# Making two of three mixed input blocks of a hybrid decoder layer in the heads' stage, and giving single weight parts their own buffers

## The chip, the cores and the metric

The kernel runs on one core of one Trainium2 chip. The metric is device time in microseconds (us) for one execution of the program. A core has five engines that this document names as the profile does: PE (the matrix multiplier, with PEld for its weight loads), DVE (vector), ACT (scalar, activation functions), POOL (general purpose; here it issues small transfers) and SP (issues the large transfers). Each engine runs its own instructions strictly in the order of its queue and waits on semaphores for the others.

## The reference

One decoder layer over 256 tokens of width 2048, all in float32. Cut to what matters here:

```python
h = _rmsnorm(x, pre_norm_g)                                  # 256 x 2048
(q_a, c_kv, k_rope, z_mla, c_in, b_gate, c_gate, z_conv,
 g_mla, g_conv) = split(h @ w_in)                            # seven of the parts are 2048 wide
...                                                          # 16 heads of latent attention
attn = attn * silu(z_mla);  y_mla = attn @ w_o_mla
u = c_gate * c_in;  conv = sum(conv_w[k] * shifted(u, k) for k in range(3))
y_conv = (b_gate * conv * silu(z_conv)) @ w_o_conv
merged = sigmoid(g_mla) * y_mla + sigmoid(g_conv) * y_conv   # the "gates" stage: g_mla, g_conv
x = x + _rmsnorm(merged @ w_out, post_norm_g)
```

## The kernel before

**Every product is three products.** The kernel keeps float32 accuracy with matrix products on rounded operands: each operand is split into `hi` (rounded, made by ACT, L282) and `lo` (the rest, made by DVE as `src - hi`, L283; both in `split_act`). A product is hi·hi + hi·lo + lo·hi, three matmuls of 128x512 on PE (`product`). The input x lives split in `x_both` (16 blocks of 128 columns, hi beside lo) for the whole run.

**Weights stream.** SP loads units of 128x2048 into `raw` (three buffers), ACT and DVE split them in halves of 1024 into `whi` and `wlo` (five buffers each), PE consumes them. `plan` lists the units in the order of use; `ahead`/`take` run the splitting one unit ahead and the loading three ahead.

**Stages.** First the latents, then the *heads' stage* (16 heads; each is interleaved with a quarter of the convolution's channels, so that PE always has `cv` matmuls to run), then the *gates and merge* stage: four products of 256x2048 by 2048x2048 (n = 0: g_mla, n = 1: g_conv, n = 2: w_o_mla, n = 3: w_o_conv), each in two halves c = 0, 1 of the output's columns, called blocks (n, c) here; then the output projection.

**The gates' blocks use seven products instead of eight.** A block runs over eight pairs k of x's blocks; each pair is a 2x2 by 2x2 block product. For pairs 0, 3 and 5 (`FAST`) of n = 0 and 1, `fast_block` makes it with seven products, which need sums of weight parts (`split_seven`: `ts` the sums, `th`/`tl` their hi and lo) and *mixed input blocks*, four differences of x's blocks for each pair (`mixed`: `xr` is x put together again from hi and lo, `xm` the four differences, `mix` their hi and lo). Products go into the PSUM banks p1, q5, q7, q6, p2, q3, q4 (the profile's `p`, `q`, `d`). Block (0, 0) runs the pairs in the order 1, 2, 4, 0, 6, 3, 5, 7 and treats only pairs 0 and 3 as fast; it is the first block after the heads' stage. The mixed blocks of pairs 0, 3 and 5 are made once, in block (0, 0), by `between(i)` before the pairs at places 1, 3 and 5, in two `ev` buffers, and are used in blocks (0, 0) to (1, 1). Units are numbered in the names: 116 is pair 0 of block (0, 0), 117 pair 6, 118 pair 3, and 121 and 124 are pairs 0 and 3 of block (0, 1). `split_seven` puts three quarters of a unit into one full and one half-filled buffer of `whi` and of `wlo`.

**What sets the order.** PE's order is the program's. On DVE and ACT a list scheduler places the instructions when the kernel is built, by its own estimate of times, but each engine then runs its queue in that fixed order.

**Small transfers.** In the heads' stage POOL issues the transposes through DRAM (`far<-via`, then `p<-far` for a head's probabilities; `far<-cw` and `at_f<-far` for gates; `cw<-cwr_dram` for the convolution's taps). `cw` is a ring of two buffers of 128x512 that stays open until n = 1. [...]

Of the kernel before, what the change touches and what calls it, by code (L numbers as in the profile page):

```python
# [11 lines left out]
F32 = mybir.dt.float32  # L12
# [3 lines left out]
ALU = mybir.AluOpType  # L16
# [68 lines left out]
def tile_layer(ctx: ExitStack, tc: tile.TileContext, xw, w0, xb, x, pos, pvec, post_g, wc, wz, wcv, wkr, wqk, wqr, wv, cwr, wd, wo, out):  # L85
# [130 lines left out]
        splits[i] = parts  # L216

    def split_seven(i, t):
        hi, hi2 = (wpool.tile([P, HALF], F32R, name=f"whi{i}_{j}", tag="whi", bufs=5) for j in range(2))
        lo, lo2 = (wpool.tile([P, HALF], F32R, name=f"wlo{i}_{j}", tag="wlo", bufs=5) for j in range(2))  # L220
        ta, tb = (sums(f"ts{i}_{j}") for j in range(2))
        ha, hb = (sums_hi(f"th{i}_{j}") for j in range(2))
        la, lb = (sums_lo(f"tl{i}_{j}") for j in range(2))
        plus = lambda o, a, b: nc.vector.tensor_tensor(o, a, b, op=ALU.add)
        two = lambda a: a.rearrange("p (j c) -> p j c", j=2)
        plus(two(ta[:, :]), two(t[:, :HALF]), t[:, 3 * R :].unsqueeze(1).to_broadcast([P, 2, R]))
        plus(tb[:, :R], ta[:, :R], t[:, R:HALF])
        plus(tb[:, R:], tb[:, :R], t[:, HALF : 3 * R])
        split_act(hi[:, :], lo[:, :], t[:, :HALF])
        split_act(hi2[:, :R], lo2[:, :R], t[:, HALF : 3 * R])  # L230
        split_act(ha[:, :], la[:, :], ta[:, :])
        split_act(hb[:, :], lb[:, :], tb[:, :])
        f = lambda a: (a[:, :R], a[:, R:])
        (b11, b22), (t1, t3), (t2, t4) = (list(zip(f(h), f(l))) for h, l in ((hi, lo), (ha, la), (hb, lb)))
        return {"b11": b11, "b22": b22, "b21": (hi2[:, :R], lo2[:, :R]), "t1": t1, "t2": t2, "t3": t3, "t4": t4}

    def ahead(i, raw=3, split=1):
        while done["raw"] < min(i + raw, len(plan)):
# [42 lines left out]
    def split_act(hi, lo, src, keep=False, later=False):  # L281
        a = nc.scalar.activation(hi, src, AF.Copy)  # L282
        b = nc.vector.tensor_tensor(lo, src, hi.bitcast(F32), op=ALU.subtract)  # L283
        if keep:

            tc.keep_in_program_order(a)
        if keep or later:
            tc.keep_in_program_order(b)
# [31 lines left out]
    main = ctx.enter_context(ExitStack())  # L320
    hp = main.enter_context(tc.tile_pool(name="hp", bufs=1))
    x_both = hp.tile([P, KD, 2 * S], F32R, name="x_both")
    cstack, astack = (main.enter_context(ExitStack()) for _ in range(2))
    cv_pool = cstack.enter_context(tc.tile_pool(name="cv_pool", bufs=1, side="right"))
    cv_f = cv_pool.tile([P, KD, S], F32, name="cv_f")
# [21 lines left out]
    def temp(name, shape=(P, S), dt=F32, bufs=2, tag=None):  # L347

        tag, n = tag or name.rstrip("0123456789_"), shape[-1]
        if n % LINE == 0:  # L350
            return (lp if tag in ("cw", "mv1x", "mv2x") else bp).tile(list(shape), dt, name=name, tag=tag, bufs=bufs)
        return bp.tile([P, -(-n // LINE) * LINE], dt, name=name, tag=tag, bufs=bufs)[:, :n]
# [84 lines left out]
    def rows(dst):  # L437
        tc.keep_in_program_order(nc.vector.tensor_tensor(dst, dst, r_x[:, :], op=ALU.mult))
# [201 lines left out]
    def group_v(v):  # L640
# [9 lines left out]
        groups["v", v] = vv  # L650
        yield

    def make(i, j, *more):
        return {"a": group_a, "r": group_r, "v": group_v}[i](j, *more)

# [187 lines left out]
    def score(h, later=False):  # L843
        made_here = scores(h)

        def rest():
            ps_by_head[h], come = made_here(later)
            coming.append(come)

        return rest if later else rest()  # L850

    for h in range(H):
        v, at = divmod(h, HV)

        if at == 0:
            for i in range(4):
                gates(v, i)
                if v == 0 and i == 0:
                    ckv_come()
                elif v == 0 and i == 1:  # L860
                    next(table_parts)
                    key_rope()
                elif v == 0 and i == 2:
                    latent_split("qa", qa, "q_g")
                elif v and i == 0:
                    arrive()
                elif v and i == 1:
                    pt = turn(ps_by_head.pop(h - 1))
                    next(tap)
                elif v and i == 2:  # L870
                    o = values(h - 1, pt)
                    next(o)
                    finish_all(make("v", v))
                    score(h)
                    finish_all(o)
            if v:
                next(tap)
            else:
                latent_split("ckv", ckv, "kv_g")
            gates_done(v)  # L880
            if v:
                arrive()
        if h == 0:

            ahead(u_grp["r", 0])
            for i in first:
                finish_all(make(*i))
        if at == 2:

            score(h)  # L890
        channels(h, 0)
        if h == 0:
            score(h)
        if at in (1, 3) and h < H - 1:
            arrive()
        if at == 0:
            coming.append(gates_turn(v, 0))
        channels(h, 1)
        if at == 0:
            arrive()  # L900
            coming.append(gates_turn(v, 1))
        else:
            pt = turn(ps_by_head.pop(h - 1))
        if h == H - 2:
            score(h + 1)

        if at == 2 or h == H - 1:
            next(tap)
        if at == 2:
            arrive()  # L910
        channels(h, 2)


        steps = [make(*i, *([at == 3] if i[0] == "a" else [])) for i in made[h]]
        if at:
            steps.append(values(h - 1, pt))
        for g in steps:
            next(g)
        if not at:
            arrive()  # L920
            if v:
                coming.append(channels_join(v - 1, 0))
        ahead_by_one = at in (0, 2) and h < H - 2
        if ahead_by_one:
            rest = score(h + 1, later=True)
        finish_all(*steps[::-1])
        if h == H - 1:
            pt = turn(ps_by_head.pop(h))
        channels(h, 3)
        if ahead_by_one:  # L930

            rest()
        if at == 2 or h == H - 1:
            next(tap)
        while len(coming) > ahead_by_one and h < H - 1:
            arrive()
        if h == H - 1:
            finish_all(values(h, pt))
        if at == 3:
            coming.append(channels_join(v, 1))  # L940
        if at == 1:
            tap = taps(v, 1)
            next(tap)
        elif at == 3 and h + 1 < H or h == H - 2:
            tap = taps(v, 0)
            next(tap)
# [20 lines left out]
        gate[n][t] = sp.tile([P, D], F32, name=f"g{n}_{t}")  # L967

    gate_tile(1, 0)
    mix = {k: sp.tile([P, 2, 4 * P], F32R, name=f"mix{k}") for k in FAST[::-1]}  # L970
    sums_lo("home")
    for t in range(NT):
        gate_tile(0, t)

# [25 lines left out]
    def split_group(place, src, c):  # L1000
        for t in range(NT):
            split_turned(src[:, c, t, :], place, c, t)

    def mixed(k):
        tmp = evens(f"xr{k}")
        f = tmp[:, :].rearrange("p (j s) -> p j s", j=2)
        ks = slice(2 * k, 2 * k + 2)
        nc.vector.tensor_tensor(f, x_both[:, ks, :S].bitcast(F32), x_both[:, ks, S:].bitcast(F32), op=ALU.add)
        raw = evens(f"xm{k}")
        a11, a21, a12, a22 = (f[:, j, t * P : (t + 1) * P] for j in range(2) for t in range(2))  # L1010
        m7, m5, m6, m3 = (raw[:, j * P : (j + 1) * P] for j in range(4))
        minus = lambda o, a, b: nc.vector.tensor_tensor(o, a, b, op=ALU.subtract)
        minus(m7, a21, a11)
        minus(m5, a21, a22)
        minus(m6, a11, m5)
        minus(m3, a12, m6)
        split_act(mix[k][:, 0, :], mix[k][:, 1, :], raw[:, :])

    def mix_part(k, j):
        return tuple(mix[k][:, o, j * P : (j + 1) * P] for o in range(2))  # L1020
# [77 lines left out]
    for n in range(2):  # L1098
        if n:
            lstack.close()  # L1100
            last_gate = spool.enter_context(tc.tile_pool(name="last_gate", bufs=1))
            gate[1][1] = last_gate.tile([P, D], F32, name="g1_1")
        for c in range(2):

            def between(i):
                if n == c == 0 and i in (1, 3, 5):
                    mixed(FAST[i // 2])
                if n == c == 1 and i in (2, 4, 6):
                    split_group(at_place, at_t, i // 2 - 1)

            outs = [[gate[n][t][:, columns(c, j)] for j in range(2)] for t in range(NT)]
            fast_block(n, c, x_part, outs, between)
            for t in range(NT):
                for o in outs[t]:
                    nc.scalar.activation(o, o, AF.Sigmoid, scale=r_col[:, t : t + 1])
# [231 lines left out]
```

## Time and profile before

| | us |
|---|---|
| median of 3 runs (1033.6 to 1034.96) | 1034.54 |
| the profiled execution, its own time | 1034.48 |
| span of its profile (first to last instruction) | 1032.7 |
| PE busy | 1022.6 (99% of the span) |
| DVE busy | 747.4 (72%) |
| ACT busy | 543.9 (53%) |
| POOL busy | 179.0 (17%) |

How to read the views: a row of the timeline has the start and the duration in us, the engine, the line, the operation, output<-input, and how many such instructions stand together (xN); the brackets behind it give the idle time of that engine just before, and what ended it. A row of the waits has the waiting operation, what it waited for, the total in us, the number of waits and the longest. A row of the windows has, for a stretch of the span, the busy time of each engine with the number of instructions in brackets, the clock granted to PE as a share of full speed, the busy share of the DMA engines and GB/s. PE's matmuls overlap in the pipeline, so a matmul's duration (0.39 us) is longer than the step from one to the next.

### The profile page before, as it was taken

The numbers are of one execution on the slowest core, as the hardware profiler recorded it, in microseconds if no ns is written. First come the engines' busy times: TensorE is split into PE (matmuls) and PEld (weight loads), VectorE is DVE, ScalarE is ACT, GpSimd is POOL, SyncE is SP. The second block draws the span as 40 slices with busy tenths as digits, with TensorE's granted clock in tenths as the row PEclk, the third lists the DMA queues.
The fourth block names the chain that finished last, engine by engine and source line by source line (L and its number), as shares of the span: only waits on it lengthen the run. The fifth ranks groups of instructions, "written<-read, shape, count | busy, mean of one in ns | idle before, by whom it ended". The sixth has DMA issues, their size and how long they took to land.

```text
span 1032.7 us, 12827 instructions
## 1 busy us (share of the span) xinstructions
PE 1022.6 (99%) x4651; PEld 851.5 (82%) x4651; DVE 747.4 (72%) x1062; ACT 543.9 (53%) x764; POOL 179.0 (17%) x344
## 2 busy tenths in 40 slices
PE   9999999999999999999999989999999999999998
PEld 7888888888888888888888868888888888888886
DVE  7588777787777777777877798898875554756572
ACT  7665545655456454564555546555654443344451
POOL 4540421104301223112133120000000000214000
PEclk9999999999999999999999989999999999999999
DMA  9775866568665676757676755555555555577852
GB/s 357 276 260 202 279 205 234 213 201 282 218 246 197 220 263 211 273 192 244 229 269 222 260 183 178 226 206 204 204 198 182 193 202 196 197 258 246 344 184 81
DMA packets 44528, 233.26 MB, mean 226 GB/s; under 512 B 7953, under 2 KB 10513, under 8 KB 21553
## 3 DMA queue, kind: packets, MB, share of 16 engines
q1 hardware_dynamic: 32400, 199.67, 54.8%
q0 software_dynamic: 11632, 29.48, 8.8%
q10 hardware_dynamic: 432, 3.29, 0.8%
q8 instruction: 36, 0.59, 0.2%
q14 instruction: 28, 0.22, 0.1%
HBM read 215.66 MB, written 12.58 MB: 221 GB/s over the span
## 4 chain that ended last, share of the span: by engine, by line
PE 97%; DVE 2%; DMA 0%; ACT 0%; issue 0%
PE cv L90 34%; PE sq L90 17%; PE q L90 8%; PE z L90 8%; PE out L90 8%; PE p L90 4%; PE d L90 2%; PE kn L90 2%; PE qa L90 2%; PE qn L90 2%; PE vv L90 2%; PE ckv L90 2%; PE sc L90 1%; PE qr L90 1%; PE o L90 1%; DVE wlo L283 1%
## 5 line engine op out<-in xcount | busy, mean ns | idle before, releaser
L283 DVE TENSOR_TENSOR wlo<-raw,whi 128x1024 fp32r<-128x1024 f32 (+1 forms) x370 | 431.8, 1179 | 202.8 <-ACT whi L282 195.4
L282 ACT ACTIVATE whi<-raw 128x1024 fp32r<-128x1024 f32 (+1 forms) x372 | 373.2, 1021 | 376.0 <-PE cv L90 116.9
L90 PE MATMUL cv<-whi,x_both 128*128 128x512 f32 x1024 | 319.8, 389 | 0.0
L90 PEld LDWEIGHTS cv<-whi,x_both 128*128 128x128 f32 x1024 | 192.3, 188 | 39.4
L90 PE MATMUL cv<-wlo,x_both 128*128 128x512 f32 x512 | 199.6, 390 | 0.0
L90 PE MATMUL sq<-whi,x_both 128*128 128x512 f32 x384 | 118.8, 389 | 0.0
L90 PEld LDWEIGHTS cv<-wlo,x_both 128*128 128x128 f32 x512 | 96.1, 188 | 19.5 <-DVE wlo L283 0.2
L90 PEld LDWEIGHTS sq<-whi,x_both 128*128 128x128 f32 x384 | 72.1, 188 | 15.0
L90 PE MATMUL z<-whi,x_both 128*128 128x512 f32 x256 | 80.0, 389 | 0.0
L90 PE MATMUL out<-whi,x_both 128*128 128x512 f32 x256 | 79.0, 389 | 0.0
L90 PE MATMUL sq<-wlo,x_both 128*128 128x512 f32 x192 | 74.7, 389 | 0.0
L367 POOL DMA_DIRECT2D far<-g x32 | 17.4, 551 | 322.5 <-DVE g L1138 289.9
L367 POOL DMA_DIRECT2D far<-via x64 | 35.2, 556 | 179.2 <-DVE via L359 178.9
L90 PEld LDWEIGHTS out<-whi,x_both 128*128 128x128 f32 x256 | 48.1, 188 | 9.9
L90 PEld LDWEIGHTS z<-whi,x_both 128*128 128x128 f32 x256 | 48.1, 188 | 9.9
L90 PE MATMUL q<-whi,x_both 128*128 128x512 f32 x168 | 55.1, 389 | 0.0
L90 PE MATMUL z<-wlo,x_both 128*128 128x512 f32 x128 | 49.8, 389 | 0.0
L90 PE MATMUL out<-wlo,x_both 128*128 128x512 f32 x128 | 49.8, 389 | 0.0
L90 PE MATMUL p<-whi,x_both 128*128 128x512 f32 x128 | 46.6, 391 | 0.0
L90 PEld LDWEIGHTS sq<-wlo,x_both 128*128 128x128 f32 x192 | 36.0, 188 | 7.4
L367 POOL DMA_DIRECT2D far<-cw x48 | 26.1, 551 | 79.1 <-DVE cw L359 79.1
L90 PE MATMUL sq<-whi,cv_first 128*128 128x512 f32 x128 | 39.7, 389 | 0.0
(253 smaller groups left out, 1433.0 us busy)
## 6 DMA issues: line engine op xcount, KB each, us to landing
raw<-wcv_dram SPq DMA_DIRECT2D x64, 1024.0 KB, 5.9
raw<-wd_dram SPq DMA_DIRECT2D x64, 1024.0 KB, 4.8
raw<-wz_dram SPq DMA_DIRECT2D x16, 1024.0 KB, 4.8
raw<-wo_dram SPq DMA_DIRECT2D x16, 1024.0 KB, 5.0
raw<-wqk_dram SPq DMA_DIRECT2D x8, 1024.0 KB, 6.1
cw<-cwr_dram POOLq DMA_DIRECT2D x24, 256.0 KB, 6.2
raw<-wc_dram SPq DMA_DIRECT2D x4, 1024.0 KB, 10.4
raw<-wv_dram SPq DMA_DIRECT2D x4, 1024.0 KB, 4.8
```

The source lines that it names most:

```text
L90: return tc.keep_in_program_order(nc.tensor.matmul(*a, **kw))
L282: a = nc.scalar.activation(hi, src, AF.Copy)
L283: b = nc.vector.tensor_tensor(lo, src, hi.bitcast(F32), op=ALU.subtract)
L367: tc.keep_in_program_order(queue.dma_start(out=f[i], in_=m))
```

## The change

Four edits:

1. `mixed` moves up in the code, takes its scratch from the caller, and is called for pairs 0 and 3 in heads 5 and 9 (`h in (HV + 1, 2 * HV + 1)`), with two `f` buffers and one `cw` buffer as scratch. x is now put together in two instructions of 128x256 rather than one of 128x512.
2. The buffers `mix0` and `mix3` (2 x 4096 bytes per partition) therefore live in `hp` through the heads' stage; the room comes from `dynamic_dma_scratch_size=8192`.
3. The third mix (pair 5, first needed in block (0, 1)) stays in block (0, 0) but moves from place 5 to place 6.
4. The half-filled `whi`/`wlo` buffers of `split_seven` are replaced by `ph`/`pl`, 128x512, two buffers each. The room is that of the two mixes, which left this pool.

```diff
     def split_seven(i, t):
-        hi, hi2 = (wpool.tile([P, HALF], F32R, name=f"whi{i}_{j}", tag="whi", bufs=5) for j in range(2))
-        lo, lo2 = (wpool.tile([P, HALF], F32R, name=f"wlo{i}_{j}", tag="wlo", bufs=5) for j in range(2))
+        hi, lo = (wpool.tile([P, HALF], F32R, name=f"{o}{i}", tag=o, bufs=5) for o in ("whi", "wlo"))
+        hi2, lo2 = part_hi(f"ph{i}"), part_lo(f"pl{i}")
...
-        split_act(hi2[:, :R], lo2[:, :R], t[:, HALF : 3 * R])
+        split_act(hi2[:, :], lo2[:, :], t[:, HALF : 3 * R])
...
     x_both = hp.tile([P, KD, 2 * S], F32R, name="x_both")
+    mix = {k: hp.tile([P, 2, 4 * P], F32R, name=f"mix{k}") for k in FAST[:2]}
...
+    def mixed(k, rows, raw):
+        xs = [rows(j) for j in range(2)]
+        for j, x in enumerate(xs):
+            h, l = (x_both[:, 2 * k + j, o : o + S].bitcast(F32) for o in (0, S))
+            nc.vector.tensor_tensor(x, h, l, op=ALU.add)
+        a11, a21, a12, a22 = (x[:, t * P : (t + 1) * P] for x in xs for t in range(2))
+        m7, m5, m6, m3 = (raw[:, j * P : (j + 1) * P] for j in range(4))
+        minus = lambda o, a, b: nc.vector.tensor_tensor(o, a, b, op=ALU.subtract)
+        minus(m7, a21, a11)
+        minus(m5, a21, a22)
+        minus(m6, a11, m5)
+        minus(m3, a12, m6)
+        split_act(mix[k][:, 0, :], mix[k][:, 1, :], raw)
...
         if h == H - 2:
             score(h + 1)
+        if h in (HV + 1, 2 * HV + 1):
+            mixed(FAST[v - 1], lambda j: temp("f")[:, :], temp("cw", (P, 512), bufs=2)[:, :])
...
-    mix = {k: sp.tile([P, 2, 4 * P], F32R, name=f"mix{k}") for k in FAST[::-1]}
-    sums_lo("home")
+    mix[FAST[2]] = sp.tile([P, 2, 4 * P], F32R, name=f"mix{FAST[2]}")
+    part_hi, part_lo = (ring(tag, F32R, R) for tag in ("ph", "pl"))
+    for r in (part_hi, part_lo, sums_lo):
+        r("home")
...
             def between(i):
-                if n == c == 0 and i in (1, 3, 5):
-                    mixed(FAST[i // 2])
+                if n == c == 0 and i == 6:
+                    tmp = evens(f"xr{FAST[2]}")
+                    mixed(FAST[2], lambda j: tmp[:, j * S : (j + 1) * S], evens(f"xm{FAST[2]}")[:, :])
...
-    nc = bacc.Bacc("TRN2", target_bir_lowering=False, num_devices=1)
+    nc = bacc.Bacc("TRN2", target_bir_lowering=False, num_devices=1, dynamic_dma_scratch_size=8192)
```

PE, POOL and SP run the same instructions in the same order as before (the two loads of `cw` that come next after a mix now wait for ACT to have read it); DVE and ACT do not. Three places on DVE follow, as the built programs have them (the name, its buffer number, the shape of the output).

The first place is DVE's queue between the heads' stage and pair 0 of block (0, 0). Before, eight rows ahead of the mix's `lo` part:

```order
L283 TENSOR_TENSOR tl116_0_5675<-ts116_0_5671,th116_0_5673 128x1024
L224 TENSOR_TENSOR ts116_1_5672<-ts116_1_5672,raw116_5622 128x512
L1012 TENSOR_TENSOR xm0_5634<-xr0_5632,xm0_5634 128x128
L224 TENSOR_TENSOR ts118_0_5758<-raw118_5712 128x1024
L283 TENSOR_TENSOR wlo117_1024_5719<-raw117_5665,whi117_1024_5718 128x1024
L1008 TENSOR_TENSOR xr3_5722<-x_both_104 128x512
L283 TENSOR_TENSOR wlo118_0_5756<-raw118_5712,whi118_0_5754 128x1024
L283 TENSOR_TENSOR tl116_1_5676<-ts116_1_5672,th116_1_5674 128x1024
L283 TENSOR_TENSOR mix0_5570<-xm0_5634,mix0_5570 128x512
```

and with the change, from the same place (the row behind the transpose `mv2`) to the last part that pair 0 needs:

```order
L224 TENSOR_TENSOR ts116_0_5686<-raw116_5646 128x1024
L283 TENSOR_TENSOR pl116_5685<-raw116_5646,ph116_5684 128x512
L224 TENSOR_TENSOR ts116_1_5687<-ts116_0_5686,raw116_5646 128x512
L283 TENSOR_TENSOR wlo117_0_5730<-raw117_5680,whi117_0_5729 128x1024
L283 TENSOR_TENSOR wlo117_1024_5734<-raw117_5680,whi117_1024_5733 128x1024
L224 TENSOR_TENSOR ts116_1_5687<-ts116_1_5687,raw116_5646 128x512
L283 TENSOR_TENSOR tl116_0_5690<-ts116_0_5686,th116_0_5688 128x1024
L283 TENSOR_TENSOR pl118_5763<-raw118_5727,ph118_5762 128x512
L283 TENSOR_TENSOR tl116_1_5691<-ts116_1_5687,th116_1_5689 128x1024
```

The rows of the mixes are gone, and so are three rows of the later pairs 6 and 3 that stood ahead of the last parts of pair 0.

The second place is DVE's queue in head 5, around its softmax (`p`, `mx`, `nb`). Before:

```order
L688 TENSOR_TENSOR p_2420<-sc5_2354,mask_122 128x256
L687 TENSOR_TENSOR p_2420<-p_2420,mask_122 128x128
L283 TENSOR_TENSOR wlo52_0_2486<-raw52_2448,whi52_0_2485 128x1024
L693 TENSOR_REDUCE mx_2426<-p_2420 128x1 x2
L694 TENSOR_SCALAR nb_2429<-mx_2426 128x2
L283 TENSOR_TENSOR wlo52_1024_2490<-raw52_2448,whi52_1024_2489 128x1024
```

and with the change:

```order
L703 TENSOR_TENSOR p_2422<-sc5_2356,mask_124 128x256
L658 TENSOR_TENSOR f_2524<-x_both_104 128x256
L661 TENSOR_TENSOR cw_2522<-f_2523 128x128
L702 TENSOR_TENSOR p_2422<-p_2422,mask_124 128x128
L283 TENSOR_TENSOR wlo52_0_2488<-raw52_2450,whi52_0_2487 128x1024
L708 TENSOR_REDUCE mx_2428<-p_2422 128x1
L661 TENSOR_TENSOR cw_2522<-f_2523,f_2524 128x128
L708 TENSOR_REDUCE mx_2428<-p_2422 128x1
L661 TENSOR_TENSOR cw_2522<-f_2523,cw_2522 128x128
L709 TENSOR_SCALAR nb_2431<-mx_2428 128x2
L283 TENSOR_TENSOR wlo52_1024_2492<-raw52_2450,whi52_1024_2491 128x1024
```

Four of the mix's seven instructions on DVE stand between these rows; the first write to `cw` waits for the four transfers `far<-cw` that read that buffer before. Head 9 reads the same.

The third place is DVE's queue at the end of block (0, 0), where it empties the PSUM banks (`g`) that block (0, 1) fills again. Before:

```order
L1050 TENSOR_TENSOR g0_0_5572<-q3_00_5579,g0_0_5572 128x512
L1050 TENSOR_TENSOR g0_1_5573<-q4_00_5580,g0_1_5573 128x512
L1050 TENSOR_TENSOR g0_1_5573<-d22_00_5581,g0_1_5573 128x512
L224 TENSOR_TENSOR ts124_0_6014<-raw124_5974 128x1024
L283 TENSOR_TENSOR wlo122_1024_5950<-raw122_5878,whi122_1024_5949 128x1024
```

and with the change:

```order
L1054 TENSOR_TENSOR g0_0_5596<-q3_00_5603,g0_0_5596 128x512
L224 TENSOR_TENSOR ts124_0_6021<-raw124_5981 128x1024
L283 TENSOR_TENSOR pl124_6020<-raw124_5981,ph124_6019 128x512
L1054 TENSOR_TENSOR g0_1_5597<-q4_00_5604,g0_1_5597 128x512
L661 TENSOR_TENSOR xm5_5852<-xr5_5851 128x128 x2
L1054 TENSOR_TENSOR g0_1_5597<-d22_00_5605,g0_1_5597 128x512
```

The first sum of unit 124, which waits for its transfer to land, and a part of it now stand ahead of two of the reads.

More of the change, by code (lines that the diff above doesn't have):

```diff
@@ L234, in split_seven @@
         (b11, b22), (t1, t3), (t2, t4) = (list(zip(f(h), f(l))) for h, l in ((hi, lo), (ha, la), (hb, lb)))
-        return {"b11": b11, "b22": b22, "b21": (hi2[:, :R], lo2[:, :R]), "t1": t1, "t2": t2, "t3": t3, "t4": t4}
+        return {"b11": b11, "b22": b22, "b21": (hi2[:, :], lo2[:, :]), "t1": t1, "t2": t2, "t3": t3, "t4": t4}
     def ahead(i, raw=3, split=1):
@@ L1002, in split_group @@
             split_turned(src[:, c, t, :], place, c, t)
[L1004 to L1017, printed above, removed]
     def mix_part(k, j):
```

## The prediction

> **What bounds the kernel now.** I read the page's busy times first, then whom PE waits for, then the windows, and last the timeline of the one place where PE stands still. The page's two rows, and all waits of PE:
>
> ```profile
> span 1032.7 us, 12827 instructions
> PE   1022.6 (99%) x4651; PEld 851.5 (82%) x4651; DVE 747.4 (72%) x1062; ACT 543.9 (53%) x764; POOL 179.0 (17%) x344
> ...
> PE q L90 <- issue: 2.3, 1, 2.3
> PE q L90 <- DVE mix L283: 1.4, 1, 1.4
> PE idle L90 <- PEq L1335: 0.8, 1, 0.8
> PE qa L90 <- ACT whi L282: 0.5, 1, 0.5
> PE fin L90 <- ACT dg L1223: 0.4, 1, 0.4
> ```
>
> PE is the bound: 99% of the span. These five are all its waits, and two of them, 3.7 of 5.4 us, stand at the matmuls `q<-th,mix`. A faster DVE or ACT elsewhere is worth nothing; only this place is. Three windows of 25 us around it, and three of 2 us inside:
>
> ```profile
> 575.00:600.00 25.00, 25.00 (x114) 20.77 (x113) 20.38 (x28) 11.88 (x14) 2.75 (x5) 1.00 0.65 218
> 600.00:625.00 25.00, 21.31 (x83) 16.66 (x82) 22.91 (x36) 13.10 (x16) 3.30 (x6) 0.86 0.53 198
> 625.00:650.00 25.00, 25.00 (x112) 20.72 (x111) 23.83 (x28) 15.68 (x19) 0.00 (x0) 1.00 0.54 184
> ...
> 608.00:610.00 2.00, 0.26 (x1) 0.29 (x2) 2.00 (x3) 1.64 (x3) 0.00 (x0) 0.87 0.80 336
> 614.00:616.00 2.00, 2.00 (x6) 1.52 (x6) 1.49 (x4) 1.53 (x2) 0.00 (x0) 0.50 0.00 0
> 616.00:618.00 2.00, 2.00 (x10) 1.62 (x9) 1.97 (x5) 1.25 (x3) 0.00 (x0) 0.92 0.00 0
> ```
>
> The stretch at 600 ran 83 matmuls where the next ran 112: 29 fewer, at 25/112 us each 6.5 us. That is more than the 3.7 us of waiting, and the clock column says why: PE's granted clock falls to 0.50 during the pause and is back only at 616. The step of a matmul at full clock is 174.08/768 = 0.2267 us (first row below), which sizes the loss; a row of the chain, then PE's timeline:
>
> ```profile
> 763.60 174.08 PE sq L90 x768
> ...
> 607.04 0.39 PE L90 MATMUL p<-whi,x_both 128*128 128x512 f32 x1
> 609.74 0.77 PE L90 MATMUL q<-th,mix 128*128 128x512 f32 x1 [2.31 <-issue]
> 612.31 1.22 PE L90 MATMUL q<-th,mix 128*128 128x512 f32 x2 [1.38 <-DVE mix L283]
> 616.32 0.39 PE L90 MATMUL p<-whi,x_both 128*128 128x512 f32 x1
> ```
>
> From 607.04 (the third product of p1 of pair 0) to 616.32 (the third of p2) lie the nine of q5, q7, q6, all `<-mix`, and three of p2: 12 steps, 2.72 us at full clock, for 9.28 us. **The loss is 6.56 us**: two pauses, and eleven matmuls at about half clock. It is all there is to win.
>
> Who is late? `mix`, made by DVE and ACT (their timelines):
>
> ```profile
> 599.83 0.66 DVE L1008 TENSOR_TENSOR xr<-x_both 128x512 f32<-128x512 f32 x1
> 600.40 1.22 DVE L224 TENSOR_TENSOR ts<-raw 128x1024 f32<-128x1024 f32 x1
> 601.53 0.49 DVE L1012 TENSOR_TENSOR xm<-xr 128x128 f32<-128x128 f32 x2
> 601.94 0.69 DVE L283 TENSOR_TENSOR wlo<-raw,whi 128x512 fp32r<-128x512 f32 x1
> 602.54 0.69 DVE L224 TENSOR_TENSOR ts<-ts,raw 128x512 f32<-128x512 f32 x1
> ...
> 611.56 0.69 DVE L283 TENSOR_TENSOR mix<-xm,mix 128x512 fp32r<-128x512 f32 x1
> ...
> 609.03 0.61 ACT L282 ACTIVATE mix<-xm 128x512 fp32r<-128x512 f32 x1
> ```
>
> ACT's hi ends at 609.64 and PE starts at 609.74 (the wait called "issue" is this one); DVE's lo ends at 612.25 and PE goes on at 612.31. DVE has no gap from 599.83 to 612.25, so it is DVE's queue, not a transfer, that is late.
>
> **The change, part by part.** From the starts of these rows DVE needs 1.13 us for a row of 1024, 0.60 for 512, 0.20 for 128.
>
> *Mixes of pairs 0 and 3 out of this queue.* The new queue (first place in the section on the change) starts where `xr` stood, at 599.83: ts 1.13, pl 0.60, ts 0.60, wlo 1.13, wlo 1.13, ts 0.60, tl116_0 1.13 gives 606.15; pl 0.60 and tl116_1 1.13 give 607.88, and some 0.09 more until it is written. PE reads `tl116_0` in the second product of q5, two steps after 607.04, at 607.50: 1.3 us to spare. It reads `tl116_1` in the second product of q6, eight steps after, at 608.85: 0.9 us to spare. ACT keeps up: before, it took its next half at 600.67, when PE freed one. From there two halves, th, and ph (0.96 each, 0.6) bring it to 604.2; th116_1 waits for its sum (605.1) and is done at 606.2, 0.5 us ahead of tl116_1's turn. So PE doesn't stop, the clock doesn't fall, and **−6.56 us**. Next late is this same tl116_1: over 0.9 us of delay on DVE would reopen the pause.
>
> *The same mixes in heads 5 and 9.* Each costs DVE 2 x 0.33 (rows of 256, below) + 4 x 0.20 + 0.60 = 2.1 us, and ACT 0.6. Two windows of the heads' stage, and POOL's and DVE's timelines in head 5:
>
> ```profile
> 225.00:250.00 25.00, 25.00 (x118) 20.93 (x117) 19.02 (x31) 13.70 (x20) 6.42 (x12) 1.00 0.77 251
> 250.00:275.00 25.00, 25.00 (x124) 21.13 (x123) 17.38 (x29) 14.08 (x24) 7.78 (x15) 1.00 0.68 234
> ...
> 248.51 0.57 POOL L371 DMA_DIRECT2D at_f<-far  x1 [6.18 <-DMA far<-cw]
> ...
> 248.76 0.41 DVE L688 TENSOR_TENSOR p<-sc,mask 128x256 f32<-128x256 f32 x1
> 249.09 0.28 DVE L687 TENSOR_TENSOR p<-p,mask 128x128 f32<-128x128 f32 x1
> ...
> 257.33 2.58 DVE L283 TENSOR_TENSOR wlo<-raw,whi 128x1024 fp32r<-128x1024 f32 x2 [1.46 <-ACT whi L282]
> ```
>
> DVE is free 13.6 of these 50 us and PE loses nothing. What hides the 2.1 us is that DVE itself waits for ACT (1.46 us in the last row, which in turn waits for PE to free a half). The new wait, the first write to `cw` behind the transfers of head 4's gate, is over when POOL goes on at 248.51; DVE comes to it after L688 and two inserted rows of 256, at about 249.8: 1.3 us to spare, with the weights' next lo queued behind it. In head 9 the same rows stand at 381.86 and 383.06, 0.5 us later on DVE's side, so 1.8 us. I take **0**; uncovered, it would be 2 x 2.1 = 4.2 us (next part), and no order of events gains here.
>
> *Pair 5's mix, one place later; ph and pl.* The mix is first read in pair 5 of block (0, 1), five units of 21 or 24 steps (some 26 us) behind that block's start, and on DVE its lo stands ahead of that pair's own weight parts, which PE needs as well: **0**. The new buffers free one half each in `whi` and `wlo`; PE waits for neither after 616: **0**, and nothing to gain. PE's own instructions are the same in number and order.
>
> *PSUM reads behind a transfer* (third place). DVE's timeline before, and the landing time of the weights' transfers:
>
> ```profile
> 639.20 0.69 DVE L1050 TENSOR_TENSOR g<-d,g 128x512 f32<-128x512 f32 x1 [0.67 <-PE d L90]
> 640.39 1.23 DVE L224 TENSOR_TENSOR ts<-raw 128x1024 f32<-128x1024 f32 x1 [0.50 <-DMA raw<-wd_dram]
> ...
> raw<-wd_dram SPq DMA_DIRECT2D x64, 1024.0 KB, 4.8
> ```
>
> Now `ts124_0` waits for its landing ahead of the reads of q4 and d22, and PE's q4 of the next block needs that bank. The landing comes 4.8 us after a buffer is free, and the queue runs some 6.5 us earlier than before, so I expect it there first. Bounds: 0, and one landing late by as much as 0.5 to 1.5 us at each of the three following block ends, 4.5 us. I take **0**, the nearer row being the 0.50.
>
> *Half the strip for POOL's descriptors.* No row shows its filling. The nearest, from the timelines of POOL and ACT and the landing times:
>
> ```profile
> 392.99 1.64 POOL L367 DMA_DIRECT2D far<-mv  x3 [2.46 <-issue]
> ...
> 564.34 0.56 POOL L371 DMA_DIRECT2D p<-far  x1
> ...
> 572.59 0.51 ACT L282 ACTIVATE pt<-p 128x384 fp32r<-128x384 f32 x1
> ...
> p<-far POOLq DMA_DIRECT2D x16, 192.0 KB, 4.4
> ```
>
> The 2.46 us is the longest pause of POOL that no wait explains. A head's `p` has 572.59 − 564.34 − 4.4 = 3.8 us of cover in head 14, so one such pause is hidden there: **0**, bounds 0 and the slow rival below. [...]
>
> **Sum.** 1034.48 (the profiled execution's own time; the median of 1034.54 is within 0.1 us of it) − 6.56 + 0 = **1027.9 us**.
>
> **The rivals.**
>
> *A. Part of it is given back in the gates' blocks* (tl116_1, or the PSUM reads). For: DVE is the fullest there, 23.83 of 25 us in the window at 625, and slacks are 0.9 us. Against: PE waits nowhere in 625 to 763 now. Price: a pause of 1 to 2 us; if it passes the length at which the clock falls, the rows above make it 6.56/3.69 = 1.8 times as dear. So 1029 to 1031.5, 1030 in the middle. [...]
>
> *B. The heads' stage doesn't hide the mixes*: 2 x 2.1 us uncovered, 1032.1; "no change" if a clock drop comes with it. Against: 13.6 free microseconds, and 1.3 us ahead of the new wait.
>
> *C. Slower: POOL's transfers stall for want of descriptor room.* For: the unexplained 2.46 us. Place: `far<-via` and `p<-far` of the heads. Most heads have more cover than head 14, for instance `p<-far` at 565.64 to its `pt` at 585.03. It decides where a head collects over two pauses of 2.46 us beyond 3.8 us; with all four `far<-via` pausing (9.8 us, 6 beyond the cover) in half the heads that is 48 us, 1076. Against: one pause in the whole run, and cover nearly everywhere.
>
> **How the numbers follow.** Forecast 1027.9, own range 1027.2 to 1029.0, chance 0.80. A 0.10, B 0.05 (half of it within 0.2%), C 0.03, and 0.02 that something unseen leaves the time where it was. About 0.2% (2 us) is what a measurement of this kernel can tell from no change. Faster by more: 0.80 + 0.10 + 0.02 = 0.92; same 0.05; slower 0.03. The range takes in the forecast's own, the spread of the runs (1033.6 to 1034.96, so 0.9 below the median) and most of A: 1026.8 to 1030.6.
>
> **What would show it.** Right: no `PE q` in the waits; some 112 matmuls and clock 1.00 in the window that holds block (0, 0); span about 1026.1; L1008 gone, rows of `f<-x_both` and `cw<-f` in heads 5 and 9 with no wait of DVE for `far<-cw`. A: PE waiting at `q` for `tl`, or at the first products of q4 for DVE's `g`. B: PE waits at `cv` between 245 and 275, or 378 and 410. C: POOL's "issue" waits grow. I am wrong if tl116_1 comes late by more than the 0.9 us, or if PE's clock falls for another reason.

## The result and the profile after

The changed kernel takes **1027.42 us** (median of 4 runs, 1027.20 to 1027.76), the kernel before 1034.07 us (4 runs, 1033.55 to 1034.96; three of them are those of the table ahead of the prediction). The ratio is 0.9935 with a 95% interval of 0.9918 to 0.9952: 6.65 us less, and by the interval between 5.0 and 8.5. The forecast was 1027.9, the range 1026.8 to 1030.6.

The profiled execution took 1027.20 us. Its page, the two rows that answer to those of before:

```profile
span 1025.4 us, 12801 instructions
PE   1019.0 (99%) x4651; PEld 849.6 (83%) x4651; DVE 745.7 (73%) x1065; ACT 543.7 (53%) x764; POOL 179.1 (17%) x344
```

All waits of PE in it (line of the waiting group, what ended the wait: us in total, times, longest):

```profile
PE idle L90 <- PEq L1340: 0.8, 1, 0.8
PE qa L90 <- ACT whi L282: 0.5, 1, 0.5
PE fin L90 <- ACT dg L1228: 0.4, 1, 0.4
```

Of the five waits of before the two at `q` are gone; the three left stand at the program's start and end. The windows of 25 us that hold block (0, 0), and two of 2 us inside (busy us and count of each engine, then the granted clock, the DMA share and GB/s):

```profile
600.00:625.00 25.00, 25.00 (x112) 20.72 (x111) 23.76 (x28) 14.63 (x16) 2.79 (x6) 1.00 0.72 275
625.00:650.00 25.00, 25.00 (x112) 20.72 (x111) 23.83 (x31) 16.55 (x20) 0.00 (x0) 1.00 0.59 207
...
608.00:610.00 2.00, 2.00 (x11) 1.65 (x10) 2.00 (x3) 0.92 (x1) 0.00 (x0) 1.00 1.08 451
...
614.00:616.00 2.00, 2.00 (x10) 1.65 (x9) 1.50 (x2) 0.73 (x2) 0.00 (x0) 1.00 0.81 246
```

112 matmuls where there were 83, at full clock throughout. The two profiled executions differ by 1032.7 − 1025.4 = 7.3 us, more than the medians do. The chain of waits splits this (start, length, what; the row of `sq` of before stands in the prediction). First before, then after:

```profile
134.77 5.47 PE cv L90 x24
```

```profile
134.06 5.47 PE cv L90 x24
...
756.31 174.08 PE sq L90 x768
```

Up to the first products of `cv` the profiled run of after is 0.71 us ahead; the start of the program varies by that much and more between the profiled executions (with pair 0's mix alone and with the twofold mixes, both below, the same row stands at 134.72 and at 135.60). From there to `sq` it is 763.60 − 134.77 = 628.83 before and 756.31 − 134.06 = 622.25 after: **6.58 us**, all between 600 and 625.

### The profile page after: what moved, and what is told of

Its sections match the earlier page's. It is cut to its first block, busy times and chain, and to the rows that moved or that the text cites. A ratio compares the mean times of both kernels' runs of the same rounds, so it can differ in the third digit from the quotient of the medians.

```text
span 1025.4 us, 12801 instructions
## 1 busy us (share of the span) xinstructions
PE 1019.0 (99%) x4651; PEld 849.6 (83%) x4651; DVE 745.7 (73%) x1065; ACT 543.7 (53%) x764; POOL 179.1 (17%) x344
## 4 chain that ended last, share of the span: by engine, by line
PE 99%; DMA 0%; ACT 0%; DVE 0%; issue 0%
PE cv L90 34%; PE sq L90 17%; PE q L90 9%; PE z L90 8%; PE out L90 8%; PE p L90 4%; PE d L90 3%; PE kn L90 2%; PE qa L90 2%; PE qn L90 2%; PE vv L90 2%; PE ckv L90 2%; PE sc L90 1%; PE qr L90 1%; PE o L90 1%; PE kr L90 0%
## 5 line engine op out<-in xcount | busy, mean ns | idle before, releaser
L283 DVE TENSOR_TENSOR wlo<-raw,whi 128x1024 fp32r<-128x1024 f32 (+1 forms) x359 | 424.1, 1194 | 205.8 <-ACT whi L282 198.7
L282 ACT ACTIVATE whi<-raw 128x1024 fp32r<-128x1024 f32 (+1 forms) x361 | 366.3, 1032 | 368.1 <-PE cv L90 113.2
L90 PE MATMUL p<-whi,x_both 128*128 128x512 f32 x106 | 37.8, 389 | 0.0
```

The costliest lines, as they stand in the source:

```text
L90: return tc.keep_in_program_order(nc.tensor.matmul(*a, **kw))
```

## The experiments

The differences are against the kernel before or the changed kernel, as each says. Each ratio is against the kernel before as it ran beside that experiment: medians 1034.09 us (19 runs), 1034.45 (25) and 1034.53 (13, for the mix of pair 3 alone and the twofold mixes).

**The strip alone.** The kernel before with one number changed, the size of the strip, which is the memory that `dynamic_dma_scratch_size` reserves:

```diff
-    nc = bacc.Bacc("TRN2", target_bir_lowering=False, num_devices=1)
+    nc = bacc.Bacc("TRN2", target_bir_lowering=False, num_devices=1, dynamic_dma_scratch_size=8192)
```

> The kernel before, with only the strip for POOL's descriptors halved to 8192 bytes; all instructions and their order stay. Theory Q (the forecast's: the whole gain is DVE's shorter queue ahead of pair 0 of block (0, 0)): the same time as before, 1034.1 within 0.5 us, the two pauses at the mix and the fall of the clock in place, POOL's longest pause that no wait explains about as before (2.5 us). Rival S (the strip itself matters, by POOL's issues): POOL's unexplained waits grow and the time moves by over 1 us, to either side.

Measured: 1034.68 us (10 runs), ratio 1.0001 (0.9991 to 1.0011). The ratio shows no effect either way. The median stands 0.1 us outside the half microsecond that was expected, well within the spread of the kernel before beside it (1033.22 to 1035.32). POOL's longest unexplained pause was not as before: it is 6.6 us, at `at_f`; the last experiment comes back to it.

**The rings alone.** The kernel before with the strip halved and the third quarters of the units (`b21` in the code) in the rings `ph` and `pl`; all mixes still in block (0, 0):

```diff
-        hi, hi2 = (wpool.tile([P, HALF], F32R, name=f"whi{i}_{j}", tag="whi", bufs=5) for j in range(2))
-        lo, lo2 = (wpool.tile([P, HALF], F32R, name=f"wlo{i}_{j}", tag="wlo", bufs=5) for j in range(2))
+        hi, lo = (wpool.tile([P, HALF], F32R, name=f"{o}{i}", tag=o, bufs=5) for o in ("whi", "wlo"))
+        hi2, lo2 = part_hi(f"ph{i}"), part_lo(f"pl{i}")
```

> The kernel before with the strip halved and the rings ph and pl, but all three mixes still made in block (0, 0). Theory Q: no gain, since DVE's queue ahead of pair 0 holds the mix as before; PE pauses at q5 for the mix's hi and lo, some 4 to 5 us in all, the clock falls, 1033.5 to 1035.5 us. Rival R (it is the rings: ph is split early and frees halves of whi, so ACT and DVE run further ahead): most of the 6.65 us, 1027.5 to 1029.5 us, and no pause at q5.

Measured: 1035.12 us (10 runs), ratio 1.0009 (0.9999 to 1.0018). No gain; both pauses at `q` are there, in PE's waits:

```profile
PE q L90 <- DVE mix L283: 2.5, 1, 2.5
PE q L90 <- issue: 2.3, 1, 2.3
```

Rival R falls.

**The mixes alone.** The changed kernel with that same piece turned back, so without `ph` and `pl` (the strip stays at 8192 bytes):

```diff
-        hi2, lo2 = part_hi(f"ph{i}"), part_lo(f"pl{i}")
...
+        hi, hi2 = (wpool.tile([P, HALF], F32R, name=f"whi{i}_{j}", tag="whi", bufs=5) for j in range(2))
+        lo, lo2 = (wpool.tile([P, HALF], F32R, name=f"wlo{i}_{j}", tag="wlo", bufs=5) for j in range(2))
```

> The changed kernel without the rings: b21's parts take halves of whi and wlo as before, the mixes of pairs 0 and 3 stay in heads 5 and 9, the strip is halved. Theory Q: the whole gain, 1027.4 within 0.5 us, no wait of PE at q5 to q6; tl116_0 and tl116_1 even earlier than with the rings (some 1 us), since pl of unit 118 no longer stands ahead of them. Rival R (it is the rings): near before, 1032 to 1034 us, since ACT has to wait for PE to free halves of whi and DVE waits for ACT.

Measured: 1027.48 us (4 runs), ratio 0.9937 (0.9922 to 0.9952): the whole gain. DVE's and PE's timelines in it (start, length, line, operation, out<-in):

```profile
603.72 2.44 DVE L283 TENSOR_TENSOR tl<-ts,th 128x1024 fp32r<-128x1024 f32 x2
...
608.30 0.39 PE L90 MATMUL q<-tl,mix 128*128 128x512 f32 x1
```

Both `tl` of pair 0 are written by 606.16, and PE reads the second at 608.30: 2.1 us to spare, against 0.9 in the changed kernel (below), where the `pl` of unit 118 stands between the two. So the rings buy no time here, and they cost 1.2 us of the slack on which the gain rests.

**Pair 0's mix alone, and pair 3's alone.** The changed kernel with one of the two mixes put back into block (0, 0):

```diff
-        if h in (HV + 1, 2 * HV + 1):
+        if h == HV + 1:
...
-                if n == c == 0 and i == 6:
+                if n == c == 0 and i in (3, 6):
```

(for pair 3's alone `h == 2 * HV + 1` and `i in (1, 6)`; the tile of the mix put back is in the gates' pool again.)

> The changed kernel with only pair 0's mix in the heads; pair 3's is made in block (0, 0) behind pair 2's start, its xr and four xm rows standing between the weights' rows ahead of tl116_1. Theory Q: DVE comes some 2 us later to tl116_1 (two rows of 256 and three of 128 and their order: 2 x 0.33 + 3 x 0.20 = 1.3 us, and the lo of unit 118 ahead of it, 1.13), against 0.9 us to spare: PE pauses 1.2 to 1.6 us at q6 of pair 0 for tl116_1. If a pause of this length leaves the clock at full, 1028.6 to 1029.0 us; if it lets the clock fall as before, 1.8 times that, 1029.6 to 1030.3 us. Rival: the slack of 0.9 us is misread and pair 3's mix is hidden too, 1027.4 us with no wait at q6; then pair 0's mix alone would have been enough.

> The changed kernel with only pair 3's mix in the heads; pair 0's is made in block (0, 0) as before, ahead of its own pair. Theory Q (the mix of pair 0 comes late because it is itself at the end of DVE's queue; pair 3's rows stand behind it): no gain, the two pauses at q5 for mix and the fall of the clock as before, 1033.5 to 1035 us. Since pair 0 alone gave 4.9 of the 6.6 us, the two parts would then not add up: each 0 and 4.9, together 6.6. Rival L (it is the sum of the rows in DVE's queue that counts, whichever pair they are of): a third or more of the gain, 1030 to 1032 us.

Measured: pair 0's alone 1029.15 us (4 runs), ratio 0.9952 (0.9937 to 0.9967); pair 3's alone 1034.25 us (10 runs), ratio 0.9996 (0.9987 to 1.0006), with both pauses at `q` (2.4 us and 1.4 us) as before. So −4.9, about nothing, and −6.65 for both: the parts don't add up, as theory Q had it, and rival L falls. Of pair 0's alone, the row of PE's waits that tells:

```profile
PE q L90 <- DVE tl L283: 1.4, 1, 1.4
```

DVE's last `tl` of the pair, from its timeline:

```profile
609.12 1.21 DVE L283 TENSOR_TENSOR tl<-ts,th 128x1024 fp32r<-128x1024 f32 x1
```

The window with the pause:

```profile
608.00:610.00 2.00, 0.97 (x5) 0.47 (x3) 2.00 (x3) 0.13 (x1) 0.00 (x0) 1.00 1.03 393
```

The mix of pair 0 is no longer late, but pair 3's rows push `tl116_1` back (written at 610.33), and PE pauses for it. The slack of 0.9 us is therefore real. The clock stays at 1.00, and the pause costs 1.73 us in the medians, about itself. The median lies between the two ranges that were set for a full and a falling clock (1028.6 to 1029.0 and 1029.6 to 1030.3), so it is the window that decides between them; the mean granted clock of all four runs is 0.999 or 1.000.

**What one pause costs.** In the changed kernel `tl116_1` is written again, once or twice, with the same numbers:

```diff
         split_act(hb[:, :], lb[:, :], tb[:, :])
+        for _ in range(1 if i == u_d[0, 0, 0] else 0):
+            nc.vector.tensor_tensor(lb[:, :], tb[:, :], hb[:, :].bitcast(F32), op=ALU.subtract)
```

(2 in place of 1 for the long pause.)

> The changed kernel with the lo of pair 0's second sum, tl116_1, made twice by DVE (one row of 1024 more); the second one stands behind ts118_0 and wlo118, so tl116_1 is last written some 3.4 us later than in the changed kernel (607.3 + 3 x 1.13 = 610.7), and PE, which wants it at 608.1, stands still once, for 2.5 us, with only that. It measures what one pause costs. Theory P (a pause of this length costs itself and no more, as the 1.41 us of mix0_alone did, 1.73 us in the medians): 1027.4 + 2.5 = 1030.0 us, clock at full in the windows behind it. Theory K (the clock falls, as before in a pause of 2.31 us, and the next eleven matmuls run at half): 1.8 times the pause and more, 1031.9 to 1032.9 us. [...]

> The same with tl116_1 made three times; the third stands behind three more rows of 1024, last written some 6.8 us later than in the changed kernel, so PE stands still once for 5.9 us. Theory P: a pause costs itself, 1027.4 + 5.9 = 1033.3 us. Theory K: the clock is at half when PE goes on and stays there for some 4 to 6.6 us, as it did before from 609.7 to 616.3, which costs half of that more: 1035.5 to 1036.7 us.

Measured: the shorter 1032.00 us (10 runs, 1029.98 to 1032.69), the longer 1036.08 us (10 runs, 1035.23 to 1036.62). The shorter one falls into both theories: two runs at 1029.98 and 1030.38, 2.6 and 3.0 us over the changed kernel; eight from 1031.44 to 1032.69, 4.0 to 5.3 over it. The mean granted clock of the whole run is 0.999 in the two and 0.997 or 0.998 in the eight. The longer one is within theory K's range, 2.8 us above theory P. PE's timeline in one of the eight:

```profile
610.80 0.50 PE L90 MATMUL q<-tl,mix 128*128 128x512 f32 x1 [2.41 <-DVE tl L234]
...
612.31 0.59 PE L90 MATMUL q<-wlo,mix 128*128 128x512 f32 x1
612.69 0.63 PE L90 MATMUL q<-whi,mix 128*128 128x512 f32 x1
613.12 0.63 PE L90 MATMUL q<-th,x_both 128*128 128x512 f32 x1
```

Windows of the same run (the last column but two is the clock):

```profile
610.00:612.00 2.00, 1.20 (x5) 1.01 (x6) 2.00 (x3) 1.19 (x2) 0.00 (x0) 1.00 0.63 266
612.00:614.00 2.00, 2.00 (x8) 1.52 (x7) 1.97 (x3) 0.64 (x1) 0.00 (x0) 0.59 0.00 0
614.00:616.00 2.00, 2.00 (x7) 1.57 (x6) 1.79 (x3) 1.47 (x2) 0.00 (x0) 0.56 0.30 33
616.00:618.00 2.00, 2.00 (x10) 1.64 (x9) 1.00 (x1) 0.00 (x0) 0.00 (x0) 1.00 0.90 365
```

PE is back at 610.80 and works at full clock; the clock falls only later. An estimate of when, from the windows: a clock of 0.59 over 2 us, if it is either 1.00 or 0.50, is full for 0.36 us and half for 1.64, so it fell at 612.36; 0.56 in the window at 614 puts its return at 615.76. From 612.69 matmuls come 0.43 us apart, against 0.23 at full clock. The median is 1032.00 − 1027.42 = 4.6 us for a pause of 2.4 in this view. The longer pause costs 8.7 us for 5.8, its clock by four windows:

```profile
610.00:612.00 2.00, 0.00 (x0) 0.00 (x0) 2.00 (x2) 1.34 (x2) 0.00 (x0) 1.00 0.74 311
612.00:614.00 2.00, 0.00 (x0) 0.00 (x0) 2.00 (x3) 0.00 (x0) 0.00 (x0) 0.80 0.00 0
...
618.00:620.00 2.00, 2.00 (x6) 1.56 (x5) 0.62 (x1) 1.44 (x2) 0.00 (x0) 0.50 1.04 442
620.00:622.00 2.00, 2.00 (x10) 1.62 (x10) 1.93 (x3) 1.30 (x2) 0.00 (x0) 0.99 0.27 33
```

By the same estimate the clock fell at 613.2 and came back at 620.04.

**How much the heads hide.** Each of the two mixes made twice, and four times, with the same result:

```diff
-            mixed(FAST[v - 1], lambda j: temp("f")[:, :], temp("cw", (P, 512), bufs=2)[:, :])
+            for _ in range(4):
+                mixed(FAST[v - 1], lambda j: temp("f")[:, :], temp("cw", (P, 512), bufs=2)[:, :])
```

> The changed kernel with each of the two mixes in the heads made four times over, the same result each time: 3 x 2.1 = 6.3 us of DVE and 1.8 us of ACT more in each of heads 5 and 9, against some 13.6 us free in 50. Theory Q (the forecast's: the heads' stage hides the mixes because DVE waits for ACT there): one mix costs nothing, and of four some 4 us a head are hidden too; what is left is at most 2 to 2.5 us a head, at the scores' first matmuls, which need kn from the same queue: 1027.4 to 1032 us. Rival B (nothing of a mix is hidden in the heads, and the gain would have been larger by two mixes' cost): 3 x 2 x 2.1 = 12.6 us more, 1040 us, and so 4.2 us of the changed kernel's time would be the mixes' own.

> The changed kernel with each of the two mixes in the heads made twice, the same result both times: 2.1 us of DVE more in each of heads 5 and 9. Theory Q (the first mix costs nothing and there is room for a second; what four cost, 5.7 us, comes from the last of them): 1027.4 within 0.5 us, no wait of PE at sc for kn. Rival B (the cover ends with the first mix): a wait of up to 2.1 us a head at sc, 1029 to 1031.6 us; a third in proportion to the four's cost would be 1.9 us, 1029.3.

Measured: four times 1033.08 us (10 runs, 1031.88 to 1034.61), twice 1027.50 us (4 runs), ratio 0.9936 (0.9922 to 0.9951). The second mix is hidden too: PE never waits for `kn`. (One of its four runs took 1028.74; it is the profiled one, with its row of `cv` at 135.60, so it lost that at the program's start.) Four mixes show where the cover ends, first in PE's waits, then in two windows behind the two pauses:

```profile
PE sc L90 <- DVE kn L283: 4.3, 2, 2.1
```

```profile
278.00:280.00 2.00, 2.00 (x11) 1.65 (x10) 0.99 (x5) 0.94 (x4) 0.47 (x1) 1.00 0.99 328
...
414.00:416.00 2.00, 2.00 (x7) 1.57 (x6) 1.51 (x6) 0.39 (x2) 1.15 (x3) 0.55 0.96 342
```

Two pauses of 2.1 us, one in each head: the place and size that theory Q gave. Its upper end of 1032 was 1.1 us too low. Part of that is the clock, which it left out: of two pauses of the same length in one execution, the first (PE back at 275.95) left the clock at 1.00 and the second (PE back at 412.63) was followed by a fall to 0.55. The ten runs lie in two groups, five from 1031.88 to 1032.59 at a mean clock of 0.999 or 1.000 and five from 1033.57 to 1034.61 at 0.998. The other part is that the first group, too, lies some 5 us above the changed kernel, where the two waits make 4.3.

**A quarter of the strip.** The changed kernel with `dynamic_dma_scratch_size=2048`.

> The changed kernel with the strip for POOL's descriptors at 2048 bytes, a quarter of the changed kernel's; instructions and order stay. Theory Q: POOL issues four to eight transfers between two waits, and the strip still has room for these: 1027.4 within 0.5 us, POOL's unexplained waits as they were (at_f 6 to 9 us off the path, far 3.2 to 3.6 in all). Rival C (POOL stalls for want of descriptor room): its unexplained waits grow in most heads, and where a head collects over 3.8 us of them p comes late to PE; 1029 us and more, to 1076.

Measured: 1027.54 us (4 runs), ratio 0.9933 (0.9918 to 0.9948). POOL's waits at `at_f` in three kernels; before:

```profile
POOL at_f L371 <- DMA far<-cw: 30.5, 7, 6.2
```

the changed kernel:

```profile
POOL at_f L372 <- DMA far<-cw: 20.6, 6, 5.5
...
POOL at_f L372 <- issue: 7.5, 1, 7.5
```

and with 2048 bytes:

```profile
POOL at_f L372 <- DMA far<-cw: 29.3, 6, 6.4
```

The 7.5 us looked like the sign that the prediction had set for rival C. But 20.6 + 7.5 = 28.1 in seven waits is what the other two have in seven and six: one wait for a landing that the profile puts down to nothing. With a quarter of the strip it isn't there at all. It goes with the size 8192: the eight kernels of that size whose waits of POOL were read each show such a wait at `at_f`, of 6.6 to 8.7 us, the strip alone among them (6.6); its rows in two of them, further down, stand in head 5, where before has 6.18 us put down to the landing. Why the profile names nothing there, and whether POOL itself adds to that wait, stays open. PE waits for none of it, and neither the halved nor the quartered strip costs time, so rival C falls.

## Why the prediction was right, step by step

**The loss of 6.56 us, and that it is all there is to win:** right. It measures 6.58 from `cv` to `sq` and 6.65 in the medians. The forecast of 1027.9 is 0.5 above the median because it started from the profiled execution (1034.48), 0.4 above the median of before with its fourth run (1034.07). That one profile gave the loss to 0.1 us is in part luck: the size of the loss differs from run to run. In the profile of the strip alone, with the same instructions as before, half clock goes on past p2: from the third product of p1 at 606.84 seventeen steps take 618.23 − 606.84 = 11.39 us, 3.85 at full clock, so the loss there is 7.5 us. All runs of before together spread over 1033.22 to 1036.05.

**DVE's shorter queue as its cause:** shown. Moving the mixes gives all of it, rings and strip none. The timelines of PE and DVE after:

```profile
606.33 0.39 PE L90 MATMUL p<-whi,x_both 128*128 128x512 f32 x1
...
608.14 0.39 PE L90 MATMUL q<-tl,mix 128*128 128x512 f32 x1
...
609.05 0.39 PE L90 MATMUL p<-ph,x_both 128*128 128x512 f32 x1
...
606.04 1.22 DVE L283 TENSOR_TENSOR tl<-ts,th 128x1024 fp32r<-128x1024 f32 x1
...
631.85 1.21 DVE L224 TENSOR_TENSOR ts<-raw 128x1024 f32<-128x1024 f32 x1
```

The twelve steps from `p` to `p`, 9.28 us before, take 609.05 − 606.33 = 2.72, as worked out. `tl116_1` is written at 607.26 and read at 608.14: 0.88 us to spare, predicted 0.9.

**The mixes in the heads at nothing:** right, with room for one more of each, but not for three. What hides them is what the step named. The `wlo` row that in the prediction waits 1.46 us for ACT starts 0.71 us earlier than before, as this whole run does, though the mix's rows now stand ahead of it; only its wait is shorter:

```profile
256.62 2.58 DVE L283 TENSOR_TENSOR wlo<-raw,whi 128x1024 fp32r<-128x1024 f32 x2 [0.62 <-ACT whi L282]
```

The step's working was wrong in one place, the margin of the new wait on `far<-cw`. For head 9 its own rows give 383.06 − 381.86 and three rows of 0.33, 2.2 us, not 1.8. And in head 5 DVE came to the wait at 248.71, not some 249.8, and before POOL went on behind the same four transfers (DVE's timeline, then POOL's row of it):

```profile
248.04 0.41 DVE L703 TENSOR_TENSOR p<-sc,mask 128x256 f32<-128x256 f32 x1
248.38 0.41 DVE L658 TENSOR_TENSOR f<-x_both 128x256 f32<-128x256 f32 x1
248.71 0.28 DVE L661 TENSOR_TENSOR cw<-f 128x128 f32<-128x128 f32 x1
...
248.94 0.57 POOL L372 DMA_DIRECT2D at_f<-far  x1 [7.52 <-issue]
```

The row of mask (L703, L688 before) starts 0.72 us earlier than before, like the whole run, and only one of the two rows of 256 stands behind it; POOL went on 0.43 us later than before. DVE does not wait, so the transfers had landed by 248.71, and POOL's row, by which the prediction measured, is not the landing. With pair 0's mix alone the two stand further apart, again with no wait of DVE:

```profile
249.38 0.28 DVE L661 TENSOR_TENSOR cw<-f 128x128 f32<-128x128 f32 x1
...
250.99 0.57 POOL L372 DMA_DIRECT2D at_f<-far  x1 [8.74 <-issue]
```

How much earlier than DVE's row the landing is, and so how near this wait is, no row shows. Had it come later, DVE's queue with the weights' lo would have stood behind it; the twofold mixes show that the queue bears 2.1 us more, but no run delayed the transfers.

**The PSUM reads at nothing:** right. `ts124_0` starts at 631.85 with no wait, so its landing came earlier, and PE runs 112 matmuls in that window.

**The new buffers at nothing:** right for the time. What the step didn't see is the 1.2 us of slack that they take.

**The price of a pause, 1.8 times its length** (rival A): right as a median at one length, wrong as a factor. 1.4 us cost 1.7; 2.4 cost 4.6 in the median, but 2.6 to 3.0 in two runs of ten; 5.8 cost 8.7. It is the pause plus, where the clock falls, the stretch of half clock (by the estimate above 3.4 us after the pause of 2.4, and 6.8 in and behind that of 5.8).

**Rivals A, B and C** did not come about. Against B the free time held, but the 1.3 us ahead of the new wait can't be read as the prediction read them. Against C the prediction counted one unexplained pause of POOL in the whole run; the timeline of before has a second, 2.25 us at 908.36, outside the heads. The runs that were made to bring A and B on gave the place that they named, PE at `q` for `tl` and PE in the heads; B's was `sc`, not `cv`. That POOL's transfers take up room in the strip, and how much, no run shows: with 2048 bytes the time is 1027.54 us, against 1027.42 with 8192, and POOL waits 29.3 us at `at_f`, against 30.5 before.

## What to carry to other kernels

Where PE is 99% busy, look for the one place where it stands still, and count the matmuls that the windows around it lack: they price a pause with its clock, which the wait alone (3.7 of 6.6 us here) does not. Work that held up a full queue in one stage cost nothing here in a stage where that queue itself waits for another engine, up to a point that doubling it finds (1027.50 us with two mixes a head, 1033.08 with four). The parts of this change don't add up, since PE waited for the latest operand alone: pair 3's mix is worth nothing alone and 1.7 us on top of pair 0's.

## What the runs showed of the hardware

Estimated as above from the windows, with a clock that is either full or half, half clock lasted from 609.48 to 616.32 before (6.8 us), from 612.36 to 615.76 after the shorter pause (3.4) and from 613.2 to 620.04 after the longer (6.8). Four more of the profiles show a fall. Their windows of 2 us give 3.4 us with the rings alone (clock 0.63 and 0.52) and with the fourfold mixes (0.55 and 0.60), and 6.8 us with the strip alone (0.85, three times 0.50, 0.94) and with pair 3's mix alone (0.76, twice 0.50, 0.53). The fall began 1.6 us after PE was back at 610.80 in the shorter pause; in the kernel before it began 2.05 us after the end of PE's last matmul (607.43) and 0.3 us ahead of PE's return at 609.74.

The single pause of 1.4 us brought no fall in 4 runs (pair 0's mix alone, 1028.69 to 1029.61 us at mean clocks of 0.999 and 1.000). The one of 2.4 us brought it in 8 of 10, by their times and mean clocks (0.997 and 0.998). What sets the beginning and the end of a fall, no run shows.

The kernel before spreads over 1033.35 to 1036.05 in 25 runs, at mean clocks of 0.995 to 0.998. The changed one, in whose profile PE has no such pause, spreads over 1027.20 to 1027.76 in its 4, at 0.999 and 1.000. That the fall of the clock makes the wider spread is argued from these numbers, not shown in each run.
